# Sums of weight quarters for Strassen's products: by VectorE, or by accumulating transfers

## The chip, the cores and the metric

The kernel runs on one core of one Trainium2 chip. Its engines work side by side: TensorE (PE, with PEld for the loading of weights), VectorE (DVE), ScalarE (ACT), GpSimd (POOL) and SyncE (SP), which here issues most transfers. POOL issues a few transfers as well. The metric is the device time of one execution in microseconds (us); lower is better. The kernel before was timed three times: a median of 2619.53 us, 2619.38 to 2621.48.

## The reference

Two layers of a streaming encoder, one step for 512 tokens of a new stream and 8 x 16 tokens of running streams, so 640 tokens of 1024 channels. Each layer is feed-forward, mixer, feed-forward, each wrapped in a residual sum and a layer norm:

```
x = layer_norm(ALPHA * x + 0.5 * swiglu(x, w_gate, w_up, w_down))
x = layer_norm(ALPHA * x + mixer(x))
x = layer_norm(ALPHA * x + 0.5 * swiglu(x, w_gate, w_up, w_down))

def swiglu(x, w_gate, w_up, w_down):
    return (silu(x @ w_gate) * (x @ w_up)) @ w_down
```

The four feed-forwards have 2816 hidden channels, 22 tiles of 128. The mixers (a state-space model beside stick-breaking attention, and a second state-space model) are not touched by the change. All is float32.

## The kernel before

The phases are ffn0, mix0, ffn1, ffn2, mix1, ffn3. Activations lie in on-chip memory twice: channel-major as a high and a low part (`xt`), token-major as the accumulator `yacc`. A product of two float32 matrices is made of three matmuls on those parts, high x high, low x high and high x low.

A weight block of 128 x 1024 (512 KB) is loaded by SP into one of four staging tiles (`raw`, `RAWS = 4`). ACT casts 512 columns of it to the high part and VectorE subtracts that from the source to get the low part (`split`, lines 86 and 87). The result is a tile of pool `w`, of which there are 11 (`UNITS = 11`); it is given back when the last matmul that reads it is done.

A feed-forward (`ffn`) makes the hidden channels of tiles 0 and 1 with plain products, and also the gate of tiles 2 and 3. After that it works on pairs of tiles with Winograd's form of Strassen's scheme. Two weight blocks are seen as the quarters A11, A12 (first block, first and second half of the model's channels) and A21, A22 (second block). The activations are seen as the quarters B11 to B22, of which the sums are made once per phase. Seven products of quarters take the place of eight (`matrix`, `product`, line 334: 12 matmuls of 128 x 320 each, 84 in a matrix). They run in the order 1, 6, 5, 2, 7, 3, 4. Three banks of the matmul memory are used per matrix: product 2 adds onto product 1's bank, so ACT first copies that one away (line 343); products 7 and 4 add onto product 6's bank, and product 3 onto product 5's, so VectorE first reads those (lines 345 and 347).

`operands` makes the seven left operands. Products 1, 2 and 4 use A11, A12 and A22 as they are. The others use sums:

```
S1 = A21 + A22 (product 5)   S2 = S1 - A11 (product 6)
S3 = A11 - A21 (product 7)   S4 = A12 - S2 (product 3)
```

SP loads the two blocks (lines 303 and 304), VectorE makes the four sums (S1 at line 317, the others at line 313) into tiles `sw` or, for S3, in the place of A21, and each operand is split.

The phase goes in rounds of four hidden tiles: gate of the first pair; the down-projection of the round before (`down`, line 119: 5 token tiles x 48 matmuls of 128 x 512, added to `yacc` at line 196); up of the first pair; gate and up of the second pair. Four matrices thus run one after another from `up` to the next round's `gate`. There are five rounds per phase and 19 pairs of blocks, 76 in all. At the end of a phase comes the layer norm; POOL has a part in it, and loads its scale and offset (line 144).

The order in each engine's queue is not the order of the code: a planner sets it when the kernel is built, by when it reckons each instruction to be ready. `tc.issue_after` forces an order on one engine; here it keeps three of the sums behind a split (`state["lo"]`). Each queue is then worked off in order. ffn0 has side work for mixer 0 between its products, on POOL and SP as well; ffn3 has that for the states of mixer 1, with many transfers on SP (lines 1004 to 1020) and small matmuls (line 1015).

Of the kernel before, what the change touches and what calls it, by code (L numbers as in the profile page):

```python
# [17 lines left out]
ALPHA = 4.0 ** 0.25  # L18
# [17 lines left out]
def kernel(ctx: ExitStack, tc: tile.TileContext, I, O, phases=PHASES):  # L36
# [58 lines left out]
    def load_w(src):  # L95
        """the two halves of a [128, 1024] block, each as its high and low part"""
        r = raw_tile()
        nc.sync.dma_start(r, src)
        u = []
        for j in range(2):  # L100
            u.append(unit())
            split(u[j][:, 0], u[j][:, 1], r[:, 512 * j:512 * j + 512])
        return u

    def w_k(w, k):
        """128 columns as stationary operand"""
# [41 lines left out]
    def layer_norm(t, g_bc, last):  # L148
        """x = LN(y) in place; y carries the residual sum over ALPHA"""
# [49 lines left out]
    def ffn(i, ph, last, side=None):  # L199
        """[A11 A12; A21 A22]: two tiles of 128 hidden channels x two halves of the model's channels;  # L200
        [B11 B12; B21 B22]: those halves x two halves of the tokens. 7 products for 8."""
        V = nc.vector
        Q = T // 2
        with ExitStack() as st:
# [5 lines left out]
            def tick(where):  # L210
                """a step of the work for the mixers, at its places in the stream of products"""
# [33 lines left out]
            for h in range(2):  # L245
                o, L = HALVES[h]
                for f in fs:
# [4 lines left out]
                    s = wk.tile([128, 512], F32, name="sw", bufs=3)[:, :L]  # L252
# [27 lines left out]
            for k in range(4):  # L280
                t1 = wk.tile([128, Q], F32, name="mx", bufs=4)
                minus(t3[:, k], "hf", (1, 1), (0, 1))
                minus(t1, "mx", (0, 1), (0, 0))
                for part in (hf32, lf32):
                    V.tensor_tensor(t2[:, k], t3[:, k] if part is hf32 else t2[:, k], quad(part, 0, 0)[:, k], op=ALU.add)
# [15 lines left out]
            def operands(src0, src1):  # L301
                r0, r1 = raw_tile(), raw_tile()
                nc.sync.dma_start(r0, src0)
                nc.sync.dma_start(r1, src1)
                a11, a12, a21, a22 = r0[:, :512], r0[:, 512:], r1[:, :512], r1[:, 512:]
                A = {p: unit() for p in PRODUCTS}

                def part(p, v):
                    state["lo"] = split(A[p][:, 0], A[p][:, 1], v).ins

                def total(o, v, w, op):
                    with tc.issue_after(state["lo"]):
                        V.tensor_tensor(o, v, w, op=op)

                # S1 = A21 + A22, S2 = S1 - A11, S3 = A11 - A21, S4 = A12 - S2
                s1, s2, s4 = (wk.tile([128, 512], F32, name="sw", bufs=3) for _ in range(3))
                V.tensor_tensor(s1, a21, a22, op=ALU.add)
                part(1, a11)
                total(s2, s1, a11, ALU.subtract)
                part(4, a22)  # L320
                total(a21, a11, a21, ALU.subtract)
                part(6, s2)
                total(s4, a12, s2, ALU.subtract)
                part(5, s1)
                part(2, a12)
                part(7, a21)
# [11 lines left out]
            def matrix(A, take):  # L338
                """take(row, column, make): make(out) writes that quarter of A B, or is the psum that holds it"""
# [5 lines left out]
                V.tensor_tensor(u, y, p1, op=ALU.add)  # L345
# [5 lines left out]
                take(1, 1, lambda o: V.tensor_tensor(o, y, v, op=ALU.add))  # L351
# [3 lines left out]
                take(1, 0, lambda o: V.tensor_tensor(o, y, p1, op=ALU.add))  # L355
# [59 lines left out]
    s5d = {}  # L415

    def s5_tables(wk):
        """Kernels of an 8-step chunk, worked out on the chip and kept in DRAM."""
# [26 lines left out]
        # sin and cos of th, 8 th, 16 th, .. 256 th, after taking out whole turns  # L445
# [17 lines left out]
        # powers a^0 .. a^8  # L463
# [10 lines left out]
        def cmul(o_r, o_i, x_r, x_i, y_r, y_i, view):  # L474
            """complex product; the operands have one shape (y may be broadcast)"""
# [17 lines left out]
        # (a_bar - 1) / a  # L493
# [13 lines left out]
        # phases of the chunk recurrence  # L507
# [19 lines left out]
        # per two pairs of groups: chunk inputs to state, state to chunk outputs, lag kernels  # L527
# [3 lines left out]
        for j in range(8):  # L531
# [20 lines left out]
            # transposed: (step, channel) on partitions  # L552
# [7 lines left out]
            # lag kernels: real part of C a^l B  # L560
# [7 lines left out]
            # state to outputs  # L568
# [13 lines left out]
        # the skip term sits on the diagonal of lag 0  # L582
# [15 lines left out]
    def mixer0(ph, last):  # L598
# [14 lines left out]
        def sigmoid_(t):  # L613
            """t holds exp(-v); leaves 1 / (1 + exp(-v))"""
# [4 lines left out]
        with ExitStack() as st:  # L619
# [20 lines left out]
            def s5_quarter(j):  # L640
# [11 lines left out]
                # chunk-major u  # L652
# [15 lines left out]
                # what each chunk adds to the state  # L668
# [34 lines left out]
                # running streams: two chunks each  # L703
# [18 lines left out]
                # outputs of the chunks  # L722
# [19 lines left out]
                # gelu (tanh form): y * sigmoid(2 sqrt(2/pi) (y + 0.044715 y^3))  # L742
# [35 lines left out]
        with ExitStack() as st:  # L778
# [17 lines left out]
            # token order reversed  # L796
# [4 lines left out]
            # rows (4 streams, 2 heads, 16 queries) of a half; new keys in reversed order: same stream, earlier key  # L801
# [57 lines left out]
            def sample(p, qT, kT):  # L859
                """4 streams at a time, queries of both heads on partitions, keys from the newest to the oldest"""  # L860
# [161 lines left out]
    def mixer1(ph, last):  # L1022
# [6 lines left out]
        with ExitStack() as st:  # L1029
            wk = pool("m1", 1, st, reuse_waits="tile")  # L1030
            psum(st, ph, a=4, b=4)
            def after_norm():
                """behind the norm that ends the phase before"""
# [6 lines left out]
            with after_norm():  # L1040
                # parameters
# [18 lines left out]
                # C of the running streams, even and odd ones apart  # L1060
# [64 lines left out]
            def gate_in(g, q):  # L1125
                """2 silu(z) of one tile"""
# [55 lines left out]
            def core_a(g, c):  # L1182
# [7 lines left out]
                # decay of the states over the block, per head (and stream)  # L1190
# [30 lines left out]
                # token-major x and B  # L1221
# [13 lines left out]
                if c == 4:  # L1235
                    # per stream: rows of 16 tokens, high|high|low parts of x against high|low|high parts of B
# [16 lines left out]
                # new state  # L1253
# [11 lines left out]
                # within the block  # L1265
# [14 lines left out]
            def core_s(g, c):  # L1280
                """running streams: 8 states, 16 tokens each; outputs token-major"""
# [71 lines left out]
            # projections of the next group and gates of this one fill the waits of the blocks  # L1353
# [73 lines left out]
def _layout(inp):  # L1427
# [6 lines left out]
    def cm(w):  # L1434
        """[K, N] -> one unit per 128 columns: [N/128, 128 k, K/128 * 128]"""
# [6 lines left out]
    def pairs(v):  # L1442
        """[32 groups, 64 states, ...] -> [(2 groups, 64 states), 16 pairs, ...]"""
# [11 lines left out]
    # mixer 0  # L1455
# [19 lines left out]
    # mixer 1: units in the order of use, per group B, C, x (4), z (4)  # L1475
# [59 lines left out]
```

## Time and profile before

| | us |
|---|---|
| median of three runs | 2619.53 (2619.38 to 2621.48) |
| profiled execution (its span, first to last instruction; no other time of it is given) | 2624.4 |
| PE busy in it | 2582.0 |
| VectorE busy | 2011.2 |
| ACT busy | 1151.1 |
| POOL busy | 242.6 |

In a row of groups stand line, engine, operation, what is written from what, shapes and count; then the busy time of the group and the mean of one in ns; then the idle time of the engine before them and what ended it. A row of waits has the engine and line that waited, what released it, the us in total, the count and the longest. The rows of the timeline begin with the start and the duration in us. Matmuls overlap, so their mean duration is longer than their distance from each other.

### The profile page before, as it was taken

The page shows a single profiled execution, that of the slowest core. Times are in us where ns is not written, and L with a number is a line of the kernel's source. Part 1 is how long each engine was busy: PE and PEld are TensorE (multiplying, and loading weights), DVE is VectorE, ACT ScalarE, POOL GpSimd, SP SyncE. Part 2 cuts the span into 40 slices and gives each one's busy share as a digit, 9 for nine tenths or more (in the row PEclk, how much of TensorE's full clock was granted, in tenths as well). Part 3 has the DMA queues.
Part 4 walks back from the last instruction along what each step waited for, and adds up shares of the span by engine and source line. Part 5 has one row for each costly group of instructions (what it writes and reads, how often), then busy time and mean ns, then how long its engine had stood idle before and what let it go on. Part 6 is the DMA issues. An engine that isn't in the chain of part 4 may idle for free. (4 is left out here: it accounts for less than half of the span.)

```text
span 2624.4 us, 41392 instructions
## 1 busy us (share of the span) xinstructions
PE 2582.0 (98%) x15657; PEld 2332.9 (89%) x15657; DVE 2011.2 (77%) x4068; ACT 1151.1 (44%) x2432; POOL 242.6 (9%) x358
## 2 busy tenths in 40 slices
PE   9999999999999999999999999999999999999998
PEld 8999999887779999998999999889989878998887
DVE  8898888664668777767976776777777789887777
ACT  5444444344634344333433343566565453343332
POOL 0000003010021000003000000411121150000001
PEclk9999999999999999999999999999999999999999
DMA  5333234542212222222222232356564622444432
GB/s 179 97 113 101 93 119 139 175 135 78 78 53 65 97 97 89 73 81 89 65 89 81 81 97 99 103 179 184 172 204 134 222 87 92 155 149 125 131 126 90
DMA packets 165751, 302.79 MB, mean 115 GB/s; under 512 B 19072, under 2 KB 89856, under 8 KB 165040
## 3 DMA queue, kind: packets, MB, share of 16 engines
q1 hardware_dynamic: 163792, 293.83, 35.1%
q0 software_dynamic: 1760, 6.33, 0.7%
q8 instruction: 123, 2.02, 0.3%
q14 instruction: 76, 0.62, 0.1%
HBM read 259.56 MB, written 40.54 MB: 114 GB/s over the span
## 5 line engine op out<-in xcount | busy, mean ns | idle before, releaser
L119 PE MATMUL bank<-w,h 128*128 128x512 f32 x2640 | 610.7, 391 | 0.0
L119 PEld LDWEIGHTS bank<-w,h 128*128 128x128 f32 x2640 | 492.3, 188 | 105.4 <-issue 3.4
L119 PE MATMUL bank<-xhi,w 128*128 128x256 f32 (+2 forms) x2528 | 562.9, 314 | 17.2 <-ACT xhi L86 7.3
L87 DVE TENSOR_TENSOR w<-raw,w 128x512 fp32r<-128x512 f32 x693 | 474.0, 696 | 106.8 <-ACT w L86 104.5
L334 PE MATMUL bank<-xhi,w 128*128 128x320 f32 x2432 | 539.8, 309 | 0.5 <-DVE w L87 0.3
L86 ACT CAST w<-raw 128x512 fp32r<-128x512 f32 x693 | 422.4, 620 | 267.2 <-PE bank L334 131.2
L119 PEld LDWEIGHTS bank<-xhi,w 128*128 128x128 f32 x2528 | 426.5, 190 | 32.8 <-issue 10.2
L334 PE MATMUL bank<-T,w 128*128 128x320 f32 x2736 | 425.1, 309 | 0.0
L334 PEld LDWEIGHTS bank<-xhi,w 128*128 128x128 f32 x2432 | 406.2, 188 | 6.4 <-issue 4.4
L334 PEld LDWEIGHTS bank<-T,w 128*128 128x128 f32 x2736 | 406.6, 188 | 0.0
L119 PE MATMUL bank<-xlo,w 128*128 128x256 f32 (+2 forms) x1264 | 393.5, 312 | 1.0 <-DVE xlo L87 1.0
L334 PE MATMUL bank<-xlo,w 128*128 128x320 f32 x1216 | 375.3, 309 | 0.0
L86 ACT CAST w<-sw 128x512 fp32r<-128x512 f32 x228 | 138.1, 620 | 463.9 <-PE bank L119 275.5
L196 DVE SCALAR_TENSOR_TENSOR yacc<-bank,yacc 128x512 f32<-128x512 f32 x240 | 164.7, 687 | 213.9 <-PE bank L119 212.4
L119 PEld LDWEIGHTS bank<-xlo,w 128*128 128x128 f32 x1264 | 241.2, 191 | 3.1 <-DVE xlo L87 1.5
L334 PEld LDWEIGHTS bank<-xlo,w 128*128 128x128 f32 x1216 | 228.0, 188 | 0.0
L87 DVE TENSOR_TENSOR w<-sw,w 128x512 fp32r<-128x512 f32 x228 | 156.1, 685 | 11.4 <-ACT w L86 11.0
L144 POOL DMA_DIRECT2D w<-in_ln_gb_dram x12 | 6.9, 576 | 1291.1 <-DVE h L87 1224.3
L119 PE MATMUL bank<-w,og 128*128 128x512 f32 x432 | 105.2, 396 | 1.7 <-DVE rs L157 0.6
L119 PEld LDWEIGHTS bank<-w,og 128*128 128x128 f32 x432 | 79.6, 188 | 19.8 <-DVE og L1331 2.2
L86 ACT CAST h<-hf 128x320 fp32r<-128x320 f32 x160 | 73.3, 459 | 48.9 <-DVE hf L371 45.2
L87 DVE TENSOR_TENSOR h<-hf,h 128x320 fp32r<-128x320 f32 x160 | 76.8, 485 | 8.1 <-ACT h L86 7.7
(397 smaller groups left out, 2924.1 us busy)
## 6 DMA issues: line engine op xcount, KB each, us to landing
raw<-in_w_gate_dram SPq DMA_DIRECT2D x88, 512.0 KB, 3.8
raw<-in_w_up_dram SPq DMA_DIRECT2D x88, 512.0 KB, 3.7
raw<-in_w_down_dram SPq DMA_DIRECT2D x88, 512.0 KB, 4.1
raw<-in_m_in_dram SPq DMA_DIRECT2D x52, 512.0 KB, 3.8
raw<-in_m_out_dram SPq DMA_DIRECT2D x24, 512.0 KB, 3.9
csb<-cs_d SPq DMA_DIRECT2D x20, 512.0 KB, 4.9
h<-in_ssd_h_dram SPq DMA_DIRECT2D x16, 512.0 KB, 5.8
h<-in_ssd_h_dram SPq DMA_DIRECT2D x32, 256.0 KB, 2.7
```

What stands on the lines that cost most here:

```text
L86: nc.scalar.copy(hi, src)
L87: return nc.vector.tensor_tensor(lo, src, hi.bitcast(F32), op=ALU.subtract)
L119: state["pe"] = nc.tensor.matmul(ps, a, b, start=(k == 0), stop=(k == n - 1)).ins
L144: nc.gpsimd.dma_start(g_bc[j], bass.AP(tensor=I["ln_gb"].tensor, offset=I["ln_gb"].offset + (2 * n + j) * D, ap=[[0, 128], [1, D]]))
L196: state["acc"] = nc.vector.scalar_tensor_tensor(ya, pb, scale, ya, op0=ALU.mult, op1=ALU.add).ins
L334: nc.tensor.matmul(ps, A[p][:, a, k * 128:k * 128 + 128], B[p][b][:, k, :], start=(first and n == 0), stop=(n == 11), skip_group_check=True)
```

## The change

The four sums are no longer made by VectorE. The signs are turned so that all four are additions: S2 = S1 + A11, S3 = A11 + A21, S4 = A12 + S2. To make up for it, the sums of the activations' quarters T3 and T1 are taken with the other sign, and so are three of the combinations of products. An addition is then a transfer that POOL issues with `accum_op=ALU.add`: the transfer engines read source and destination and write the sum to the destination.

Per pair SP loads the second block into `r1`, A11 into S2's tile, the first block into `r0`, and A11 into S3's tile. POOL adds A22 from memory onto A21 (S1, in `r1`), S1 onto S2's tile, A21 from memory onto S3's tile, and S2 onto A12 (S4, in `r0`, once A12 has been split). The pool `sw` has four tiles for three. The sums' `issue_after` goes with them, and the parts are split in the order 1, 2, 4, 5, 6, 7, 3 in the code. The comments that the change also drops are left out below.

```diff
             def operands(src0, src1):
                 r0, r1 = raw_tile(), raw_tile()
-                nc.sync.dma_start(r0, src0)
-                nc.sync.dma_start(r1, src1)
-                a11, a12, a21, a22 = r0[:, :512], r0[:, 512:], r1[:, :512], r1[:, 512:]
+                s2, s3 = (wk.tile([128, 512], F32, name="sw", bufs=4) for _ in range(2))
+                s1, s4 = r1[:, :512], r0[:, 512:]
                 A = {p: unit() for p in PRODUCTS}
+
+                def plus(o, v):
+                    nc.gpsimd.dma_start(o, v, accum_op=ALU.add)
 
                 def part(p, v):
-                    state["lo"] = split(A[p][:, 0], A[p][:, 1], v).ins
-
-                def total(o, v, w, op):
-                    with tc.issue_after(state["lo"]):
-                        V.tensor_tensor(o, v, w, op=op)
+                    split(A[p][:, 0], A[p][:, 1], v)
 
-                s1, s2, s4 = (wk.tile([128, 512], F32, name="sw", bufs=3) for _ in range(3))
-                V.tensor_tensor(s1, a21, a22, op=ALU.add)
-                part(1, a11)
-                total(s2, s1, a11, ALU.subtract)
-                part(4, a22)
-                total(a21, a11, a21, ALU.subtract)
-                part(6, s2)
-                total(s4, a12, s2, ALU.subtract)
-                part(5, s1)
-                part(2, a12)
-                part(7, a21)
+                nc.sync.dma_start(r1, src1)
+                nc.sync.dma_start(s2, src0[:, :512])
+                nc.sync.dma_start(r0, src0)
+                plus(s1, src1[:, 512:])
+                nc.sync.dma_start(s3, src0[:, :512])
+                part(1, r0[:, :512])
+                part(2, r0[:, 512:])
+                plus(s2, s1)
+                plus(s3, src1[:, :512])
+                part(4, r1[:, 512:])
+                part(5, s1)
+                part(6, s2)
+                plus(s4, s2)
+                part(7, s3)
                 part(3, s4)
                 return A
...
-                minus(t3[:, k], "hf", (1, 1), (0, 1))
-                minus(t1, "mx", (0, 1), (0, 0))
-                for part in (hf32, lf32):
-                    V.tensor_tensor(t2[:, k], t3[:, k] if part is hf32 else t2[:, k], quad(part, 0, 0)[:, k], op=ALU.add)
+                minus(t3[:, k], "hf", (0, 1), (1, 1))
+                minus(t1, "mx", (0, 0), (0, 1))
+                V.tensor_tensor(t2[:, k], quad(hf32, 0, 0)[:, k], t3[:, k], op=ALU.subtract)
+                V.tensor_tensor(t2[:, k], t2[:, k], quad(lf32, 0, 0)[:, k], op=ALU.add)
...
-                V.tensor_tensor(u, y, p1, op=ALU.add)
+                V.tensor_tensor(u, p1, y, op=ALU.subtract)
...
-                take(1, 1, lambda o: V.tensor_tensor(o, y, v, op=ALU.add))
+                take(1, 1, lambda o: V.tensor_tensor(o, y, v, op=ALU.subtract))
...
-                take(1, 0, lambda o: V.tensor_tensor(o, y, p1, op=ALU.add))
+                take(1, 0, lambda o: V.tensor_tensor(o, y, p1, op=ALU.subtract))
```

More of the change, by code (lines that the diff above doesn't have):

```diff
@@ L251, in ffn @@
                             [(xh[:, k, o:o + L], xl[:, k, o:o + L]) for k in range(KT)])
-                    s = wk.tile([128, 512], F32, name="sw", bufs=3)[:, :L]
+                    s = wk.tile([128, 512], F32, name="sw", bufs=4)[:, :L]
                     state["silu"] = nc.scalar.activation(s, pg, AF.Silu).ins
@@ L302, in operands, with part @@
                 r0, r1 = raw_tile(), raw_tile()
-                nc.sync.dma_start(r0, src0)
-                nc.sync.dma_start(r1, src1)
-                a11, a12, a21, a22 = r0[:, :512], r0[:, 512:], r1[:, :512], r1[:, 512:]
-                A = {p: unit() for p in PRODUCTS}
-                def part(p, v):
-                    state["lo"] = split(A[p][:, 0], A[p][:, 1], v).ins
-                def total(o, v, w, op):
-                    with tc.issue_after(state["lo"]):
-                        V.tensor_tensor(o, v, w, op=op)
-                s1, s2, s4 = (wk.tile([128, 512], F32, name="sw", bufs=3) for _ in range(3))
-                V.tensor_tensor(s1, a21, a22, op=ALU.add)
-                part(1, a11)
-                total(s2, s1, a11, ALU.subtract)
-                part(4, a22)
-                total(a21, a11, a21, ALU.subtract)
+                s2, s3 = (wk.tile([128, 512], F32, name="sw", bufs=4) for _ in range(2))
+                s1, s4 = r1[:, :512], r0[:, 512:]
+                A = {p: unit() for p in PRODUCTS}
+                def plus(o, v):
+                    nc.gpsimd.dma_start(o, v, accum_op=ALU.add)
+                def part(p, v):
+                    split(A[p][:, 0], A[p][:, 1], v)
+                nc.sync.dma_start(r1, src1)
+                nc.sync.dma_start(s2, src0[:, :512])
+                nc.sync.dma_start(r0, src0)
+                plus(s1, src1[:, 512:])
[6 more added lines that the diff above has]
+                part(5, s1)
                 part(6, s2)
-                total(s4, a12, s2, ALU.subtract)
-                part(5, s1)
-                part(2, a12)
-                part(7, a21)
+                plus(s4, s2)
+                part(7, s3)
                 part(3, s4)
```

## The prediction

> **What bounds the kernel now.** I first read the busy shares on the profile's page, then what the matrix engine waits for.
>
> ```profile
> span 2624.4 us, 41392 instructions
> PE 2582.0 (98%) x15657; PEld 2332.9 (89%) x15657; DVE 2011.2 (77%) x4068; ACT 1151.1 (44%) x2432; POOL 242.6 (9%) x358
> PE bank L119 <- ACT xhi L86: 7.3, 6, 3.1
> PE bank L334 <- DVE w L87: 0.3, 1, 0.3
> L334 PE MATMUL bank<-xhi,w 128*128 128x320 f32 x2432 | 539.8, 309 | 0.5 <-DVE w L87 0.3
> ```
>
> PE is busy 98% of the span. Its longest group of waits (line, releaser, us in total, times, longest) is 7.3 us, for transposed activations at the borders of phases. The seven products (L334) waited 0.5 us in the whole run. So the operands which the change makes in another way arrive in time already. The chain of work that ended last, cut to one round of the last feed-forward phase, and the busy times of the second phase (430 us) and of that round (81 us) say the same:
>
> ```profile
> 2469.51 12.51 PE bank L334 x84
> 2482.45 12.51 PE bank L334 x84
> 2495.38 12.50 PE bank L334 x84
> 2508.31 12.51 PE bank L334 x84
> core 0: us, PE busy (x) PEld busy (x) DVE busy (x) ACT busy (x) POOL busy (x), PEclk, DMA share, GB/s
> 800.00:1230.00 430.00, 426.66 (x2543) 399.83 (x2542) 323.45 (x595) 172.31 (x323) 21.23 (x18) 1.00 0.25 83
> 2427.00:2508.00 81.00, 81.00 (x464) 72.93 (x464) 63.10 (x113) 29.81 (x57) 0.00 (x0) 1.00 0.42 136
> ```
>
> A matrix of 84 matmuls starts every 12.94 us, so one of its seven products takes 1.85 us; there is no hole between matrices. VectorE, which the change relieves, is at 323.45/430 = 75% and 63.10/81 = 78%: loaded, but not what the end waits for.
>
> **What is removed.** Per pair of weight blocks VectorE makes four sums of 128x512. There are 76 pairs:
>
> ```profile
> L317 DVE TENSOR_TENSOR sw<-raw 128x512 f32<-128x512 f32 x76 | 52.1, 686 | 5.5 <-DMA raw<-in_w_up_dram 4.9
> L313 DVE TENSOR_TENSOR sw<-sw,raw 128x512 f32<-128x512 f32 x76 | 51.9, 683 | 0.0
> L313 DVE TENSOR_TENSOR sw<-raw,sw 128x512 f32<-128x512 f32 x76 | 51.8, 682 | 0.0
> L313 DVE TENSOR_TENSOR raw<-raw 128x512 f32<-128x512 f32 x76 | 51.8, 682 | 0.0
> ```
>
> That is 304 instructions and 52.1 + 51.9 + 51.8 + 51.8 = 207.6 us, so VectorE should fall from 2011 to about 1803 us. On the path this is worth at most what L334 waits for VectorE, 0.5 us; I count 0, because PE's own 12.94 us per matrix hides all of it. The sign changes swap add for subtract, one for one, in the sums of X and in the combining of products: same count, same shapes, 0 us.
>
> **What is added.** Per pair: two more loads of 256 KB on SP (A11 into S2's and S3's tile) and four accumulating transfers of 256 KB issued by POOL; in all 152 and 304. Nothing accumulates in this trace. The nearest rows are the other transfers that POOL issues (512 KB each), the matching loads by SP in that round, and the software queue's total:
>
> ```profile
> L144 POOL DMA_DIRECT2D w<-in_ln_gb_dram x12: 527/551/661, 418.9 to 2586.7; - x12
> DMA to landing us min/median/max: 3.8/5.7/8.5
> raw<-in_w_up_dram SPq DMA_DIRECT2D x4, 512.0 KB, 4.0
> q0 software_dynamic: 1760, 6.33, 0.7%
> ```
>
> POOL's issue takes 0.55 us: 304 x 0.55 = 167 us of an engine that stands at 242.6 us, off the path. SP's 152 x 0.33 us (its rows below) is 50 us beside waits. From issue to landing, L: an accumulation moves half of a 512 KB transfer, but must also read its destination. Low end 3.8 us (the fastest 512 KB copy), high end 2 x 5.7 = 11.4 us (as if read and added in two transfers); I take 5.7 us, since source plus destination are again 512 KB read.
>
> For the engines that carry the transfers: 83 GB/s go with a share of 0.25. The additions to one round of four matrices are 4 x 512 KB loaded and 4 x 1 MB accumulated, 6.3 MB in 81 us or 78 GB/s, a share of about 0.23; counting accumulations double, 0.39. The last phase would go from 0.42 to 0.65 or 0.81. That is not full on average; loads and landings will lengthen in bursts.
>
> **When the sums are due.** This decides the result. SP, ACT and VectorE around the same matrix:
>
> ```profile
> 2425.16 0.33 SPq L303 DMA_DIRECT2D raw<-in_w_up_dram  x1
> ...
> 2433.01 0.37 SPq L304 DMA_DIRECT2D raw<-in_w_up_dram  x1
> 2433.48 0.38 SPq L303 DMA_DIRECT2D raw<-in_w_gate_dram  x1
> 2436.39 0.33 SPq L304 DMA_DIRECT2D raw<-in_w_gate_dram  x1
> ...
> 2466.48 0.33 SPq L303 DMA_DIRECT2D raw<-in_w_up_dram  x1
> 2467.72 0.49 SPq L304 DMA_DIRECT2D raw<-in_w_up_dram  x1
> ```
>
> ```profile
> 2464.42 0.62 ACT L86 CAST w<-sw 128x512 fp32r<-128x512 f32 x1 [22.02 <-PE bank L119]
> 2465.10 1.29 ACT L86 CAST w<-raw 128x512 fp32r<-128x512 f32 x2
> 2471.51 0.43 ACT L343 COPY mx<-bank 128x320 f32<-128x320 f32 x1 [0.78 <-PE bank L334]
> 2473.74 0.68 DVE L87 TENSOR_TENSOR w<-sw,w 128x512 fp32r<-128x512 f32 x1
> ```
>
> Call the four matrices U (2469.51), G (2482.45), U2 (2495.38) and G2 (2508.31). Their weights are loaded 27 to 46 us ahead (G: 2433.48 to 2482.45; U2: 2467.72 to 2495.38). What gates the splits into high and low parts is not the weights but the 11 split tiles: ACT's cast at 2464.42 waited 22.02 us for a matmul to give one back. So for U and G the chain load, S1, S2 has 30 us and more and costs nothing.
>
> U2 is the tightest. S4 = A12 + S2 is added into U's staging tile, after A12 was split (cast to 2466.4, VectorE 0.68: 2467.1), and lands at 2467.1 + 5.7 = 2472.8. Part 4 and part 5 of U give back the tile of U2's A21/A22 by about 2470; its load lands 4.0 later, 2474. S2's own tile comes back when S4 has landed: A11 loaded by 2476.8. Then S1 at 2474 + 5.7 = 2479.7, S2 at 2485.4, split (0.62 + 0.68) at 2486.7. Product 6 is the second of U2 and starts at 2495.38 + 1.85 = 2497.2: 10.5 us to spare over two landings, so L may reach 10.9. S4 of U2 lands near 2491.1, its part is done at 2492.4, and product 3, the sixth, starts at 2495.38 + 5 x 1.85 = 2504.6. The cover is thus split tiles waiting for PE. If it were gone, each further us of two landings would cost PE 2 us.
>
> This supposes that POOL issues by readiness. Were it to take the code's order, S1 of the next pair would stand behind S4 of this one, which waits for a landing; each pair would hold POOL for 2 L + 4 x 0.55 = 13.6 us, against 12.94 of a matrix. I take readiness, because the first rows show that a queue isn't in the code's order: the two loads of one pair, adjacent in the code, are issued 7.9 us apart with others between.
>
> **The sum.** 0 (sums leave VectorE) + 0 (signs) + 0 (transfers, under the split tiles' wait) on the profiled span of 2624.4 us. That execution is given by its span alone; it stands 4.9 us (0.19%) above the median of the three runs, 2619.53 us, which I predict unchanged: 2620 us. This comparison can tell about 0.2%, 5.2 us, from no change; the engine that sets the end has no 5 us to win in these stages.
>
> **Rivals.**
>
> A, slower: POOL's queue is held by S4 in the code's order. U2's S2 then lands at 2467.1 + 5 x 0.55 + 4 L and must be there 1.3 us before 2497.2: L up to 6.5; G2's at 2467.1 + 8 x 0.55 + 6 L, 1.3 us before 2510.2: L up to 6.2. From there each us of L costs 6 us per round. At L = 7.0: 6 x 0.8 = 5 us in each of 20 rounds, about 96 us, 2715 us; at 8.5 six times 2.3, 276 us, 2895 us. For it: the chain is longer than anything on POOL now. Against it: the loads' order above, and half the bytes of the 5.7 us row.
>
> B, slower: a cast waiting for a late sum stands in ACT's queue (or its subtraction in VectorE's) ahead of reading a product. ACT's copy at 2471.51 must be over before product 2 writes the same bank at 2469.51 + 3 x 1.85 = 2475.1: 3.6 us, less 0.43 for the copy, leaves 3.2. If a sum is later than its place in the queue by more than 3.2 us, PE loses the rest, in up to 76 matrices: at 4.2 us late 76 us, 2696 us. For it: VectorE is full in U (its rows follow one another). Against it: splits wait for tiles more than for sums.
>
> C, slower: POOL cannot write a transfer's descriptors while VectorE works. VectorE is at 75 to 78%; if issue had to wait for four VectorE instructions (2.7 us) each time, L would be 8.4, and with POOL's queue in the code's order it would end near A's 2895 us; in order of readiness under 10.9, with no loss. Against it: twelve issues took 527 to 661 ns within such stretches. The Trainium skill (SBUF — State Buffer, section "SBUF: two separate sides") warns of this: a transfer issued from GpSimd of about 620 ns took about 3100 ns beside a VectorE copy. Its section "Who interferes with whom" exempts the two-input instruction that VectorE mostly runs here; by that, and by the 527 to 661 ns, the rule should not bite.
>
> D, slower: transfers crowd the last phase (share 0.65 to 0.81, above 0.9 in bursts), and the state work there gets its loads late. Only one phase of four: 5 rounds x 4 us = 20 us, 2640 us.
>
> E, faster: VectorE's relief reaches PE after all. All waits in the PE rows for feed-forward are under 8 us; 6 us won would be 2614 us.
>
> **How the numbers follow.** No change 0.52; A 0.13; B 0.15; C 0.05; D 0.10; E 0.05. Slower is A + B + C + D = 0.43. The range reaches on the low side to E's 2614, and on the high side past B to A's smaller price, 2715; left out are A's and C's larger prices. No change by itself is 2614 to 2625.
>
> **What would show it.** Right: the four VectorE sum rows are gone and VectorE is near 1803 us; 304 POOL transfers land in about 5.7 us; matrices still start 12.94 us apart; the waits of L334 stay under 2 us. Wrong: holes before product 6 or 3 released by a cast or subtraction that waits for a transfer (A if POOL is held by S4, B if ACT's or VectorE's queue is), POOL issues well above 0.7 us (C), longer landings in the last phase alone (D). A landing above 10.9 us, or POOL in the code's order, makes the prediction wrong.

## The result, and the profile after

The kernel after takes 2745.84 us (median, 2740.42 to 2747.51), the kernel before 2619.45 us (median of four). The ratio is 1.0464, with a 95% interval of 1.0442 to 1.0485: 4.6% slower; the two medians divided give 1.0483, inside that interval. Forecast were 2620 us, no change, and a range up to 2715 us. So the time lies above the range. In two experiments below a few executions took far longer than the rest (one of 5116.74 us with the tile of S4's own, two of 2800.15 and 2804.52 us in the last); the ratios leave them out, the medians do not.

The page of the kernel after, with its busy times and two of its groups (the rows as described before), and the row of the kernel before that answers to the first group:

```profile
span 2738.7 us, 42516 instructions
PE 2618.8 (96%) x15657; PEld 2360.0 (86%) x15657; DVE 1850.7 (68%) x3764; ACT 1146.2 (42%) x2432; POOL 506.5 (18%) x662
L335 PE MATMUL bank<-T,w 128*128 128x320 f32 x2736 | 448.7, 319 | 72.3 <-DVE hf L352 57.2
L309 POOL DMA_DIRECT2D raw<-sw x76 | 82.1, 1080 | 100.0 <-DVE w L87 83.4
```

```profile
L334 PE MATMUL bank<-T,w 128*128 128x320 f32 x2736 | 425.1, 309 | 0.0
```

The span grew by 2738.7 - 2624.4 = 114.3 us, and the first two rows split it in two. PE's time outside its busy time grew from 42.4 to 119.9 us: **77.5 us of stops**. Its busy time grew from 2582.0 to 2618.8 us for the same 15657 matmuls: **36.8 us of slower matmuls**. The products with sums of activations (T) carry most of both: 72.3 us idle before them where there was none, and 448.7 us busy where it was 425.1 (a mean of 319 ns for 309). VectorE did become freer, by 160.5 us, and gained nothing by it.

What PE waits for in the seven products (line, releaser, us in total, times, longest):

```profile
PE bank L335 <- DVE hf L352: 57.2, 24, 5.1
PE bank L335 <- DVE s L352: 15.0, 10, 3.2
```

Line 352 is VectorE's reading of the bank in which product 7 was added to product 6 (line 351 before). Product 4 adds onto that bank and cannot start until it is read. These 34 waits are 72.2 of the 77.5 us. The feed-forward phases in four windows (the columns as in the prediction):

```profile
70.00:485.00 415.00, 390.15 (x2262) 362.08 (x2261) 287.31 (x688) 160.47 (x317) 89.83 (x99) 0.97 0.63 161
827.00:1283.00 456.00, 435.74 (x2560) 406.85 (x2561) 286.24 (x525) 172.87 (x327) 88.00 (x95) 0.99 0.58 145
1283.00:1745.00 462.00, 442.07 (x2585) 412.54 (x2585) 289.00 (x529) 171.59 (x328) 89.31 (x96) 0.98 0.58 143
2268.00:2730.00 462.00, 442.00 (x2475) 395.64 (x2473) 312.42 (x565) 153.93 (x297) 74.12 (x83) 0.99 0.68 180
```

The second and third phase each hold 20 us in which PE did nothing, at a mean DMA share of 0.58; before, the second held 3.3 us, at 0.25. One stop, step by step, in the second phase, where the up matrix U of a round starts at 1127.65. The timeline of ACT, POOL, VectorE and PE:

```profile
1123.13 0.62 ACT L86 CAST w<-raw 128x512 fp32r<-128x512 f32 x1 [21.51 <-PE bank L119]
1125.17 3.34 ACT L86 CAST w<-raw 128x512 fp32r<-128x512 f32 x5
1129.58 0.89 POOL L309 DMA_DIRECT2D raw<-sw  x1
1131.37 0.62 ACT L86 CAST w<-sw 128x512 fp32r<-128x512 f32 x1 [0.81 <-PE bank L335]
1137.80 1.14 ACT L86 CAST w<-raw 128x512 fp32r<-128x512 f32 x2 [5.81 <-DMA raw<-sw]
1138.45 0.69 DVE L87 TENSOR_TENSOR w<-raw,w 128x512 fp32r<-128x512 f32 x1 [4.83 <-ACT w L86]
1139.06 0.48 DVE L374 TENSOR_TENSOR hf<-bank,s 128x320 f32<-128x320 f32 x1
1140.48 0.48 DVE L352 TENSOR_TENSOR hf<-bank,mx 128x320 f32<-128x320 f32 x1
1141.02 2.23 PE L335 MATMUL bank<-T,w 128*128 128x320 f32 x7 [2.65 <-DVE hf L352]
```

The third of the five casts in ACT's row 1125.17 is that of A12 of the **next** matrix, G; it comes so late because split tiles came back only with the end of the down-projection's matmuls, for which ACT stood 21.51 us. (These are 120 in a round, 24 for each of the five token tiles and not the 48 named further up.) It and its subtraction release G's S4, which POOL issues at 1129.58 and whose cast starts 8.2 us later. ACT stands from 1131.99 to 1137.80 for it. VectorE has the subtraction of the same split next and stands 4.83 us. Behind it waits the readout of U that product 4 needs. It was due when product 3 ended, at about 1138.4. It came at 1140.48, and PE lost 2.65 us.

No product needed this S4 yet. The numbers of the buffers in the engines' queues, laid against the trace, give the times below for four stops (us from the span's start). A plain count agrees: the trace has 76 transfers `raw<-sw` and 76 matrices, and the transfer issued at 1129.58 is the 33rd, as G is the 33rd matrix.

```
A12 cast  S4 issued  S4 cast   PE goes on (stop)   product 3 reads S4
  882.2     886.6      894.8      898.1 (4.83)          910.2
 1126.5    1129.6     1137.8     1141.0 (2.65)         1154.4
 1342.0    1345.2     1353.6     1356.9 (3.73)         1369.9
 1589.8    1592.6     1601.1     1604.3 (2.64)         1616.5
```

The cast of S4 came 15 to 17 us ahead of its use each time. In 21 of the 23 stops over 1 us in the seven products, ACT had stood 2.7 to 8.3 us for the landing of an S4, until 2.3 to 6.2 us before PE went on. The other two, of 1.6 and 1.9 us, lie in the last phase.

What took the other 36.8 us is in the windows of PE alone around that stop (PE busy, granted clock, DMA share, GB/s):

```profile
1134.00:1138.30 4.30, 4.30 (x30) 1.00 1.01 200
1138.40:1141.00 2.60, 0.00 (x0) 0.87 0.81 183
1141.10:1147.00 5.90, 5.90 (x22) 0.50 0.90 206
1148.00:1154.00 6.00, 6.00 (x43) 1.00 0.69 170
```

After the stop TensorE has half its clock: 22 matmuls in 5.90 us, then 43 in 6.00. A stop of 2.65 us thus costs some 3 us more behind it. The mean granted clock, 0.981 after and 0.994 before, says the same of the whole run: 2738.7 x 0.019 - 2624.4 x 0.006 = 36.3 us.

The landings (median us from issue) and the row of ACT's waits that names the cause:

```profile
sw<-raw POOLq DMA_DIRECT2D x76, 256.0 KB, 4.4
raw<-sw POOLq DMA_DIRECT2D x76, 256.0 KB, 5.4
sw<-in_w_up_dram POOLq DMA_DIRECT2D x40, 256.0 KB, 5.7
```

```profile
ACT w L86 <- DMA raw<-sw: 221.9, 41, 12.1
```

Two windows of the round shown, before U and after S4's issue (us, POOL busy, granted clock, DMA share, GB/s), say why that landing took 8 us and not 5:

```profile
1106.00:1127.00 21.00, 1.22 (x2) 1.00 0.21 43
1129.60:1137.70 8.10, 2.61 (x3) 1.00 0.99 210
```

The DMA engines stand at 0.21 while everything waits for split tiles, and are full as soon as these come back.

### The profile page after: what moved, and what is told of

Same layout as the page of the kernel before. It is cut to its first block, busy times and chain, and to the rows that moved or that the text cites. A ratio compares the mean times of both kernels' runs of the same rounds, so it can differ in the third digit from the quotient of the medians.

```text
span 2738.7 us, 42516 instructions
## 1 busy us (share of the span) xinstructions
PE 2618.8 (96%) x15657; PEld 2360.0 (86%) x15657; DVE 1850.7 (68%) x3764; ACT 1146.2 (42%) x2432; POOL 506.5 (18%) x662
## 4 chain that ended last, share of the span: by engine, by line
PE 32%; DMA 9%; DVE 5%; issue 4%; ACT 2%; POOL 1%; SPq 0%; POOLq 0%; DVEq 0%; ACTq 0%
PE bank L119 20%; PE bank L335 9%; DMA raw<-sw 4%; DMA raw<-in_w_up_dram 1%; DVE w L87 1%; DMA h<-in_ssd_h_dram 1%; DMA sw<-in_w_gate_dram 1%; ACT w L86 1%; DMA sw<-in_w_up_dram 1%; DMA csb<-cs_d 1%; DVE acc L1108 0%; PE bank L1270 0%; PE bank L1294 0%; PE bank L1256 0%; DMA ext<-z_d 0%
## 5 line engine op out<-in xcount | busy, mean ns | idle before, releaser
L86 ACT CAST w<-raw 128x512 fp32r<-128x512 f32 x769 | 465.5, 619 | 793.7 <-PE bank L119 297.7
L87 DVE TENSOR_TENSOR w<-raw,w 128x512 fp32r<-128x512 f32 x769 | 525.2, 695 | 255.6 <-ACT w L86 253.6
L335 PE MATMUL bank<-T,w 128*128 128x320 f32 x2736 | 448.7, 319 | 72.3 <-DVE hf L352 57.2
L335 PEld LDWEIGHTS bank<-T,w 128*128 128x128 f32 x2736 | 423.0, 195 | 82.1 <-DVE hf L352 64.0
L87 DVE TENSOR_TENSOR w<-sw,w 128x512 fp32r<-128x512 f32 x152 | 104.3, 689 | 44.8 <-ACT w L86 44.2
L309 POOL DMA_DIRECT2D raw<-in_w_up_dram x40 | 35.3, 882 | 475.1 <-DVE w L87 266.9
L309 POOL DMA_DIRECT2D sw<-raw x76 | 67.2, 884 | 280.7 <-DMA raw<-in_w_up_dram 85.1
L86 ACT CAST w<-sw 128x512 fp32r<-128x512 f32 x152 | 94.4, 622 | 43.8 <-ACT w L86 23.8
L309 POOL DMA_DIRECT2D raw<-sw x76 | 82.1, 1080 | 100.0 <-DVE w L87 83.4
```

The costliest lines, as they stand in the source:

```text
L86: nc.scalar.copy(hi, src)
L87: return nc.vector.tensor_tensor(lo, src, hi.bitcast(F32), op=ALU.subtract)
L309: nc.gpsimd.dma_start(o, v, accum_op=ALU.add)
L335: nc.tensor.matmul(ps, A[p][:, a, k * 128:k * 128 + 128], B[p][b][:, k, :], start=(first and n == 0), stop=(n == 11), skip_group_check=True)
```

## The experiments

The theory: casts and subtractions of a late S4 stand in the queues ahead of readouts, and S4 is late because it is added in place onto A12, which must be split first. The rivals: POOL's queue holds the sums up; the transfers crowd out other work; VectorE or the turned signs cost time. Some expectations below call the S4 that is late that of U. The numbered queues, laid against the trace only later, show that it is G's, the next matrix's. That changes the name, not what the runs tell apart.

All ratios are to the kernel before, with 95% intervals. "Not busy" is the span less PE's busy time, 42.4 us in the profile before and 119.9 after.

**S4 by VectorE, the other three by transfer.**

```diff
-                plus(s4, s2)
+                V.tensor_tensor(s4, s4, s2, op=ALU.add)
```

> S1, S2 and S3 stay accumulating transfers (228 of the 304), S4 = A12 + S2 is made by VectorE again (76 sums, about 52 us of VectorE). Queue theory (ACT's cast of S4 stands in ACT's queue ahead of the readouts of products and waits 222 us for S4's transfer; PE's 75 us of idle time and the half clock after it follow from that): the waits of L335 for L352 fall from 72 us to under 10 us, the clock goes back to about 0.99, 2620 to 2635 us. Traffic theory (transfers and POOL's descriptors slow the engines as such): three quarters of the loss of 126 us stay, about 2715 us. Chain theory (S1 and S2 are late as well): 2680 us or more.

2638.77 us, ratio 1.0054 (1.0033 to 1.0074), a little above the 2635 us expected. Nearly nine tenths of the loss are gone with one of four sums. The first three phases have no wait in the seven products any more. The rest sits in the last phase (not busy in the whole run: 55.3 us):

```profile
PE bank L335 <- DVE hf L352: 5.5, 3, 3.2
PE bank L335 <- DVE s L352: 4.6, 5, 1.2
```

**S4 alone by transfer**, S1 to S3 by VectorE, without the two extra loads.

```diff
+                V.tensor_tensor(s3, r0[:, :512], r1[:, :512], op=ALU.add)
+                V.tensor_tensor(s1, s1, r1[:, 512:], op=ALU.add)
+                V.tensor_tensor(s2, r0[:, :512], s1, op=ALU.add)
...
                 plus(s4, s2)
```

> Only S4 is an accumulating transfer (76), the other three sums are on VectorE and the extra loads of A11 are gone. Queue theory: ACT still waits for S4 ahead of the readouts, but POOL's queue holds nothing ahead of S4, so each wait is about 3 us shorter: a part of the loss, 2630 to 2690 us, with DMA raw<-sw still the main releaser of ACT. Traffic theory: a quarter of the loss, about 2650 us, spread without that wait. Chain theory: 2620 to 2630 us.

2640.9 us, 1.0066 (1.0051 to 1.0081). With no other sums under way S4 lands in 3.6 us (median) for 5.4. ACT and PE still wait for it, but less long:

```profile
PE bank L333 <- DVE hf L350: 10.1, 5, 3.7
ACT w L86 <- DMA raw<-sw: 72.9, 27, 4.2
```

So S4's place makes the stops possible, and the crowd of the other transfers makes the landings long enough for most of them.

**POOL's order**: S1 of the next pair is issued after S4 of this one.

```diff
-                plus(s1, src1[:, 512:])
+                with tc.issue_after(state["s4"]) if "s4" in state else ExitStack():
+                    plus(s1, src1[:, 512:])
...
-                plus(s4, s2)
+                state["s4"] = plus(s4, s2).ins
```

> As changed, but POOL may issue S1 of a pair only after S4 of the pair before. Queue theory: S4 of the first up matrix of a round is issued 2 to 3 us earlier, so its landing and PE's stall move by as much: 2660 to 2710 us. If the order in POOL's queue doesn't matter, or the traffic theory holds: 2740 to 2750 us.

2748.76 us, 1.0481 (1.0462 to 1.05): no gain. This expectation failed. In that round G's S4 is now the first that POOL issues. It lands after 4.8 us, ACT stands only 1.42 us for it, and U has no stop. But the sums behind it get later: ACT stands 6.01 us for the S4 of U2, and it is G that stops, for 2.32 us. Over the whole run the stops in the products are longer than in the change, 83.6 us for 72.2, and spread to the reading of product 6 (mx):

```profile
PE bank L336 <- DVE hf L353: 42.5, 18, 4.9
PE bank L336 <- DVE s L353: 27.3, 14, 5.8
PE bank L336 <- DVE mx L347: 8.6, 5, 2.6
```

So POOL's order settles which sum is late; the loss stays, and it is not the cause.

**The split of S4 later in the queues**: POOL as in the last kernel, and the split of S4 stands behind ACT's copy and VectorE's reading of product 6 of the matrix that uses it.

```diff
-                part(3, s4)
+                A["late"] = lambda: part(3, s4)
...
-                nc.scalar.copy(p1, x)
+                c = nc.scalar.copy(p1, x).ins
...
-                V.tensor_tensor(u, p1, y, op=ALU.subtract)
+                r = V.tensor_tensor(u, p1, y, op=ALU.subtract).ins
+                with tc.issue_after(c), tc.issue_after(r):
+                    A["late"]()
```

> As the run with POOL's order, and the split of S4 is queued on ACT behind the copy of product 1 of its own matrix, and on VectorE behind the reading of product 6, so that it can't stand ahead of a readout of the matrix before. Queue theory: the stalls at L352 go, 2620 to 2650 us, with what is left at the first up matrix of a round, where S4 lands last. Traffic theory: no change, 2740 to 2750 us.

2661.27 us, 1.0143 (1.0123 to 1.0163), above the 2650 us expected. The same transfers, issued in the order of the kernel just seen; only the place of a cast and a subtraction in two queues is another. The time falls by 87 us, and ACT no longer waits for S4. What is left is the next sum in line, S2:

```profile
ACT w L86 <- DMA sw<-raw: 61.9, 39, 5.7
```

The queue's order is thus shown to be what turns a late transfer into a stop.

**The traffic alone**: all sums by VectorE; in the second and third phase two loads and four accumulations per pair go to tiles that nobody reads.

```diff
+                  q0, q1 = (wk.tile([128, 512], F32, name="scr", bufs=4) for _ in range(2))
+                  nc.sync.dma_start(q0, src0[:, :512])
+                  nc.sync.dma_start(q1, src0[:, :512])
+                  plus(q0, src1[:, 512:])
+                  plus(q1, src1[:, :512])
+                  plus(q0, q1)
+                  plus(q1, q0)
```

> All four sums are made by VectorE, with the turned signs. In ffn1 and ffn2 (the phases with room for scratch tiles) each pair also issues two loads of 256 KB and four accumulating transfers of 256 KB on scratch tiles that no engine waits for. Queue theory: transfers that nobody waits for cost nothing, ffn1 and ffn2 together stay within 4 us of the 868 us that they take before (first matmul after the border to the same of the next phase), 2618 to 2630 us. Traffic theory: those two phases lose what the change loses there, 49 us, 2660 to 2675 us. The other two phases show the turned signs alone: 0 us.

2787.27 us, 1.0639 (1.0614 to 1.0665). This missed, and it doesn't measure what it was made for: the loads to the scratch tiles stood in SP's queue until POOL's chain gave a tile back, and the weights behind them came late:

```profile
SPq L318 <- DMA scr<-scr: 322.7, 49, 17.6
```

It is the same mechanism on a third queue. The traffic by itself stayed open until the run with a tile of S4's own.

**A late readout without any transfer**: all sums by VectorE; in the first up matrix of a round, in the second and third phase, 8 additions into an unused tile stand ahead of the readout.

```diff
+                if late:
+                    for _ in range(8):
+                        with tc.issue_after(r):
+                            r = V.tensor_tensor(idle, idle, idle, op=ALU.add).ins
+                with tc.issue_after(r):
+                    take(1, 1, lambda o: V.tensor_tensor(o, y, v, op=ALU.subtract))
```

> No accumulating transfers at all; all sums on VectorE. In ffn1 and ffn2, in the first up matrix of each round (10 in all, 8 or more of them with a round before), eight idle additions of 128x512 (5.5 us) stand in VectorE's queue between the reading of product 5 and the first readout after product 7. Queue theory: PE stops before product 4 for 1 to 4 us in each, as in the changed kernel, and the clock is halved for 3.4 us or more after stops of 2.4 us and longer: 10 to 40 us of idle time and 5 to 20 us by the clock, 2635 to 2680 us. If halved clocks come from the transfers and not from the stops: no halved clock in these phases beside their borders, 2630 to 2660 us.

2626.21 us, 1.0026 (1.001 to 1.0041), no stop over 1 us in the products: a miss. VectorE had room for 8 additions. The run is still of use: it has the turned signs and none of the transfers, and with all its 80 additions it costs 0.1 to 0.4%, which stands at the edge of what can be told from no change.

**The same with 18 additions.**

```diff
-                    for _ in range(8):
+                    for _ in range(18):
```

> No transfer accumulates: all sums are made by VectorE. In the first up matrix of each round of the second and third phase, 18 additions (about 12 us of VectorE) into a tile that nobody reads stand ahead of the first readout of products, where 8 of them had brought no stop. If a stop of TensorE by itself halves the granted clock for some us: stops of 2 to 6 us in eight to ten matrices, a half clock of 3 to 7 us behind those of over 2.4 us, and 2640 to 2700 us. If the half clock belongs to the accumulating transfers: the stops without any half clock, the granted clock at 0.99 as before. If VectorE's slack covers these too: no stop, 2620 to 2630 us.

2675.26 us, 1.019 (1.0169 to 1.0212). Now there are stops, with no accumulating transfer in the kernel. The windows of PE in its trace (PE busy, granted clock, DMA share, GB/s):

```profile
865.10:868.10 3.00, 0.01 (x1) 1.00 0.41 153
868.90:872.30 3.40, 2.90 (x12) 0.50 0.02 5
953.90:957.30 3.40, 1.87 (x11) 1.00 0.00 0
958.90:962.30 3.40, 3.40 (x26) 1.00 0.02 5
```

A stop of 3.03 us, then 3.4 us of half clock. Two stops of 1.4 and 1.5 us (the third window holds the second of them) leave the clock at 1.00. The half clock therefore belongs to the stop, not to the transfers.

**S1 and S3 by transfer**, S2 and S4 by VectorE.

```diff
-                plus(s2, s1)
+                V.tensor_tensor(s2, r0[:, :512], s1, op=ALU.add)
...
-                plus(s4, s2)
+                V.tensor_tensor(s4, s4, s2, op=ALU.add)
```

> Only S1 and S3, which add weights from memory and depend on no other sum, are accumulating transfers (152); S2 and S4 are made by VectorE. Queue theory: the chain is one landing deep and starts 27 us or more ahead, so no wait ahead of a readout: 2618 to 2630 us, VectorE about 104 us below before. Chain theory: sums from transfers are late whatever their depth, 2640 us or more.

2650.08 us, 1.0121 (1.0105 to 1.0137): slower than with S2 by transfer too (1.0054), which I had not expected; the time is in the range named for the chain theory. VectorE itself now waits for a landing, S1's, with readouts behind it:

```profile
DVE sw L320 <- DMA raw<-in_w_up_dram: 59.1, 24, 4.5
```

**A tile of its own for S4**: all four sums by transfer, as in the change, but in the second and third phase S4 is added onto a second copy of A12. That is one load of 256 KB more per pair.

```diff
+                if ph in ("ffn1", "ffn2"):
+                    s4 = wk.tile([128, 512], F32, name="sx", bufs=2)
...
+                if ph in ("ffn1", "ffn2"):
+                    nc.sync.dma_start(s4, src0[:, 512:])
```

> As changed, but in ffn1 and ffn2 (the phases with room for it) S4 is added onto a copy of A12 in a tile of its own (one more load of 256 KB), so it no longer waits until A12 is split. Queue theory: S4 lands before the split tiles are given back, ACT's waits for it end there, and ffn1 and ffn2 together lose under 12 us in place of 49; 2695 to 2715 us in all. If S4's lateness comes from POOL's queue or from the landing itself and not from that wait: the loss stays, 2740 to 2755 us.

2700.88 us, 1.0302 (1.0272 to 1.0331). What is left of the loss lies in the first and the last phase, where S4 is still made in place: 31.8 and 22.9 us of waits in the seven products, and none in the two phases between. Those two, in windows:

```profile
836.00:1268.00 432.00, 429.40 (x2560) 402.60 (x2560) 288.52 (x522) 174.23 (x326) 87.31 (x94) 1.00 0.65 163
1268.00:1704.00 436.00, 432.25 (x2584) 405.34 (x2584) 292.86 (x530) 174.21 (x328) 89.51 (x97) 1.00 0.65 163
```

PE is busy to within 4 us, and the clock is at 1.00. From the first matmul of a phase to that of the next it is 432.8 and 435.5 us, where the kernel before has 432.7 and 435.5. Yet more is moved than in the change, and the DMA engines are as full behind the start of U (1121.95 here; the columns as in the two windows above):

```profile
1121.00:1129.00 8.00, 1.75 (x2) 1.00 0.95 282
1129.00:1140.00 11.00, 1.75 (x2) 1.00 0.99 253
```

In this round G's S4 is issued at 1107.1, where the change had to wait until 1129.6, and its cast waits for a split tile, not for a transfer:

```profile
1127.42 0.62 ACT L86 CAST w<-sx 128x512 fp32r<-128x512 f32 x1 [1.14 <-PE bank L339]
```

**The tile in three phases, S4 by VectorE in the first** (where memory is full).

```diff
-                if ph in ("ffn1", "ffn2"):
+                if ph in ('ffn1', 'ffn2', 'ffn3'):
                     s4 = wk.tile([128, 512], F32, name="sx", bufs=2)
...
+                if ph in ('ffn0',):
+                    V.tensor_tensor(s4, s4, s2, op=ALU.add)
+                else:
+                    plus(s4, s2)
```

> In the second to fourth feed-forward phase S4 is added onto a copy of A12 in a tile of its own (one more load of 256 KB per pair); in the first, where no memory is left for the tile, S4 is made by VectorE; S1 to S3 are accumulated everywhere. If S4's wait for the split of A12 in the shared tile is the cause of the stops: no stop in the first three phases, VectorE's and ACT's queues never hold a readout back there, and the time is within 1% of before, 2618 to 2645 us; what is left would come from the last phase, where the transfers crowd the state work (share of the DMA engines 0.7 or more). If S1 to S3 cost time by themselves, as the run with S1 and S3 alone suggested (2650 us): 2650 us or more, with stops in all phases.

2649.07 us, 1.0098 (1.0078 to 1.0117), between the two expectations. Three phases are free of stops in the products. In the last one 446 us hold 20 us in which PE does nothing, at a DMA share of 0.71. There VectorE waits for loads of the mixer's state, and ACT for S4 in its own tile:

```profile
DVE h L1033 <- DMA h<-in_ssd_h_dram: 31.0, 14, 4.8
ACT w L86 <- DMA sx<-sw: 11.5, 4, 4.1
```

The row of that phase of the kernel before that answers to the first:

```profile
DVE h L1018 <- DMA h<-in_ssd_h_dram: 1.6, 2, 1.1
```

**No sum late**: the tile in the second and third phase, S4 by VectorE in the first, all four sums by VectorE in the last.

```diff
-                if ph in ('ffn1', 'ffn2', 'ffn3'):
+                if ph in ('ffn1', 'ffn2'):
...
+                if ph in ('ffn3',):
+                    V.tensor_tensor(s3, r0[:, :512], r1[:, :512], op=ALU.add)
+                    V.tensor_tensor(s1, s1, r1[:, 512:], op=ALU.add)
+                    V.tensor_tensor(s2, r0[:, :512], s1, op=ALU.add)
+                else:
+                    plus(s1, src1[:, 512:])
```

> S4 on a copy in its own tile in the second and third phase, S4 by VectorE in the first, all four sums by VectorE in the last. If S4's place is the cause and TensorE sets the time: no stop from sums anywhere, 2618 to 2628 us, the same as before, though VectorE is some 130 us less busy. If VectorE's relief were worth anything on the path: under 2614 us. If accumulating transfers cost time wherever they are made: over 2640 us.

2623.06 us, 0.9993 (0.9979 to 1.0007): the time of the kernel before. All of the loss is accounted for by the last phase's transfers and by S4; that its place is the cause is shown for the second and third phase, while in the first S4 was taken off the transfers altogether. The relief of VectorE is worth nothing measurable on the path:

```profile
PE 2584.6 (98%) x15657; PEld 2336.2 (89%) x15657; DVE 1911.4 (73%) x3859; ACT 1153.6 (44%) x2432; POOL 422.1 (16%) x567
```

PE is as busy as before, with VectorE 100 us less busy. No version found beats the kernel before. With PE at 98% and no waits in the products there is little to win here.

## Why the prediction was wrong, and where it was right

**The sums leave VectorE: 0 on the path.** Right, by the last run. The busy time fell by 160.5 us, not by the 207.6 us of the rows added up. VectorE's instructions overlap at their ends: rows of 0.68 us start 0.60 us apart, and 304 x 0.60 is 182 us. What the other 22 us are stays open.

**Signs: 0.** Right: the last run carries them at a ratio of 0.9993.

**The landing L.** Medians of 4.4 to 5.7 us for the taken 5.7 (3.2 to 9.0 us in all), and 8.1 us for G's S4 in U, under the limit of 10.9. The bounds were good. But I worked with one L for all times. The averages of 0.48 to 0.64 for the DMA share hide the shape of a round: 0.21 in the 21 us before U, 0.99 in the 8 us after S4's issue. The same split tiles for which everything waits come back at once, and then loads and sums all start.

**POOL.** An issue took 0.87 us on average (263.9 us more for 304), not 0.55. Off the path, as supposed. POOL's queue is neither in the code's order nor by readiness: the planner had fixed it, and S1 of the next pair, issued at 1128.70, stood just ahead of G's S4. The run that turned the two gained nothing.

**The step that failed is the third zero of the sum: transfers under the split tiles' wait.** The section on due times asked when the matrix needs a sum, and there it was right: S4 of U, of G and of U2 were split 11 to 17 us before product 3, and no product waited for its own operand. It did not ask where the cast of that sum stands in ACT's queue, and what is behind it. For U and G it followed the chain only through S1 and S2. S4 has to wait for A12's split, and that for a split tile. The wait which was to be the cover is what makes S4 late. A12 of G was cast at 1126.5, just before U began at 1127.65, and the cast of S4 started 11 us later, with U's readouts in the same queues.

**Rival B was the mechanism**, at a chance of 0.15, with the argument "splits wait for tiles more than for sums" set against it. That argument spoke for it. That its sizes came near is luck. Its slack of 3.2 us was that of ACT's copy ahead of product 2; what came late is VectorE's reading ahead of product 4. Its price was 1 us in 76 matrices, 76 us; the run has 34 waits with a mean of 2.1 us, 72.2 us: half the number at twice the length. What B lacked altogether was the 36.8 us of half clock behind the stops; with it, 2620 + 76 + 37 is 2733 us, against a profiled 2738.7, and past the range's upper end of 2715 us.

**The other rivals.** A: no; the run with POOL's order has A's order, and there too PE stopped ahead of readouts, not for operands. C: no; the longest of the 304 issues took 1.61 us, and the 3.1 us of which the Trainium skill warns (SBUF — State Buffer, section "SBUF: two separate sides") did not come. D: true for the last phase. The run with S4 by VectorE waits there 21.6 us for the loads of the mixer's state (1.6 before). Its 1.0054, less the last run's 0.9993, is some 16 us, where I had 20; neither has a stop in the products of the first three phases, but they differ there too, so this is an estimate. E: no.

**The test I named was too narrow.** A landing over 10.9 us or POOL in the code's order was to make the prediction wrong; neither came. The other sign that I named did come: holes released by ACT's and VectorE's queues. In the change they lay at product 4, since it waits for a readout, and not before 6 or 3, which wait for operands.

## What to carry to other kernels

When work moves from an engine to a transfer, ask of each instruction that consumes the result where it stands in its engine's queue and what stands behind it; that it is early for its consumer is not enough. An in-place sum inherits the wait of the operand's other reader, here a split that waits for a tile, and a copy of its own took that away at the price of one more load. As an estimate from the table below, price a stop of TensorE of 2.4 us or more at its length plus half of the 3 to 7 us after it.

## What the runs showed of the hardware

TensorE's clock. I took the stops of six of these kernels (the change, and the runs with POOL's order, the later split, the own tile, the tile in three phases, and 18 additions), and whether a half clock begins between the stop's start and 2 us after its end:

```
stop of PE      stops   with half clock after
1.0 to 1.9 us     75       4
1.9 to 2.4 us     16       4
2.4 to 2.75 us    23      14
over 2.75 us      48      44
```

The half clock lasts 3.4 or 6.8 us, rarely longer. The Trainium skill ("TensorE: Matmul & The Clock Gate", section "What's actually happening") puts the return to half rate after an idle window of about 3.4 us that runs freely. The lengths of 3.4 and 6.8 us agree with such a window. The stops don't: here 2.4 us were often enough, and a stop need not fill a window of 3.4 us.

The clock records of all 13 traces say what decides. In each trace all half clocks begin on one grid of 3.413 us, to within 2 ns, so the window does run freely. And it is the idle share of a window of this grid that counts, not the length of a stop. The table takes windows at full clock, with PE idle as the trace shows it, and leaves out the first 30 us and the stretch of 570 to 760 us in mixer 0:

```
PE idle in the window   windows   with half clock in the next
under 40%                  8957       0
40 to 55%                    91       9
55% and more                105     104
```

The stop of 2.65 us above left PE idle for 57% of one window (1136.91 to 1140.32) and 20% of the next. The clock was halved at 1140.32 and stayed so for two windows. A halved window with 15% or more of idle time was always followed by another (62 of 62). In that stretch of mixer 0 half clocks also begin behind windows in which the trace shows PE busy throughout; why is open.

In the second and third phase of these kernels, accumulating transfers of 256 KB cost, by themselves, nothing on the path at a mean DMA share of 0.65, with bursts of 0.99, as long as no queue held a readout behind their landing.
